# Rate of a convolution's taps and hold of three transposes in a decoder layer on one core

## The chip, the cores and the metric

The kernel runs on one core of a Trainium2 chip. The metric is device time in microseconds. Three runs of the kernel before took 1584.47 to 1587.35 us, with a median of 1585.04.

## The reference

One decoder layer on 256 tokens of width 2048, in float32:

```python
h = rmsnorm(x, g_mix); proj = h @ w_in
u_glu, q_da, k_da, v_da, q_xa, gate_pre = split(proj)
# branch A
u = a * sigmoid(b)                       # a, b: halves of u_glu, 1024 channels each
u = causal depthwise conv of u (31 taps) + b_dw
y_conv = silu(layernorm(u, g_ln, b_ln)) @ w_conv_out
# branch B: differential attention, 4 heads, rotary; branch C: cross-attention into rmsnorm(mem)
y_da = (...) @ w_da_out;  y_xa = (...) @ w_xa_out
merged = g0 * y_conv + g1 * y_da + g2 * y_xa      # g: sigmoid(gate_pre)
x = x + merged @ w_mix_out
x = x + square(relu(rmsnorm(x, g_mlp) @ w_up)) @ w_down     # d_ff 8192
out = rmsnorm(x, g_final)
```

## The kernel before

Every weight matrix is read once, in blocks of 256 rows by 512 columns. `produce` (L306) loads a block (`raw`, on SP's queue), ScalarE rounds it to `whi`, and VectorE makes the rest, `wlo`. There are four buffers of each. Activations are kept transposed and split in the same way (class `Act`), so that a product is three matmuls: hi by whi, hi by wlo, lo by whi (L346 to L348). A `group` (L334) multiplies one activation by 512 columns of a weight: 8 steps of one block each for 2048 rows, 4 for 1024. A step is 2 k-tiles by 2 token halves by 3 matmuls, 12 of 128x512. Up to three further blocks are produced ahead of the step at hand. Before the products of a k-tile the group calls `finish` on the task that makes that tile of the activation (L367), which issues whatever the task has left.

Side work is written as generators, the tasks, in four lanes ("t", "conv", "a0", "a1"). At the end of a step `side_step` (L137) gives the first task of each lane one `tick`. A tick adds the task's rate to its credit, and each whole unit of credit runs the task to its next yield. A task with hold=1 starts one unit short, so its first tick issues nothing (L86). A finished task leaves its lane, and the next one starts.

The lane "conv" carries, in this order, `conv_half(0)`, spawned at the end of the second w_in group, `conv_half(1)`, spawned at the end of the fourth (both at rate CONV_RATE), and `conv_norm` at NORM_RATE = 1 (L627). `conv_half` (L509) transposes its half of u through TensorE in four steps and then takes 31 steps of four VectorE operations, one tap on four channel blocks each. The taps are tied behind the last product issued so far (`later`, L525). `conv_norm` (L528) is the layer norm over channels and the swish: two reductions, a matmul with ones (`pm`), eight subtractions, eight squares with seven additions, a second matmul (`pvar`), square root, reciprocal and a Newton step, eight scalings, and for each of the eight channel blocks a sigmoid, an affine activation, their product and its split into cvT's hi and lo parts. It has 31 yields.

The order of the groups: four of w_in (the convolution's input), four of w_mem_kv, two of w_in for the cross-attention's q, four for q and k, two for v. Then, for each of four column chunks c: three gate groups, and the three branch outputs w_xa_out, w_da_out and w_conv_out (4 steps each), which read xaT, daT and cvT. The branch outputs are merged on VectorE (`products`, L879). Then four groups of w_mix_out on mT, and four times four groups of w_up on x1T and four of w_down on ff.

`to_parts_dve` (L248) turns a chunk of 512 columns round with 16 VectorE transposes of 32x256 in four steps, tied behind the last `wlo` issued (L245), and splits it in two more. It is spawned with HOLD = 1 for each merged chunk (L894), each chunk of x1 (in `x1_task`, L929) and each relu chunk (L959). The merged and x1 chunks are made by VectorE, the relu chunks by ScalarE (relu and square). When the last chunk of four is spawned, the very next group needs it at its seventh step of eight.

A planner orders each engine's instructions when the program is built, by the order of issue and a model of when each is ready. It may draw an instruction ahead of its place if nothing ties it.

```python
CONV_RATE = 0.6
...
            conv_tasks.append(spawn(conv_half(g), "conv", CONV_RATE))
...
    t_norm = spawn(conv_norm(), "conv", NORM_RATE)
    cvT.tasks = [t_norm] * 8
...
                finish(act.tasks[k + c])
```

Of the kernel before, what the change touches and what calls it, by code (L numbers as in the profile page):

```python
# [27 lines left out]
EPS = 1e-6  # L28
G = 512
KB = 2  # L30
CONV_RATE = 0.6
NORM_RATE = 1.0
WARM = 10
WB = 4
AHEAD = 3
HOLD = 1
LAMBDA_INIT = 0.8 - 0.6
NEG = -3.0e38
VECS = (("g_mix", 16), ("g_mem", 16), ("g_mlp", 16), ("b_dw", 8), ("g_ln", 8), ("b_ln", 8), ("g_sub", 2))
# [68 lines left out]
def decoder_layer_kernel(  # L108
# [19 lines left out]
    def spawn(gen, lane="t", rate=1.0, hold=0):  # L128
        t = Task(gen, rate, hold)
        lanes[lane].append(t)  # L130
        return t
# [64 lines left out]
    def both(f):  # L196
        seen = []

        def g(t, ps):
            seen.append(ps)  # L200
            if len(seen) == NT:
                f(seen)

        return g
# [13 lines left out]
    def scaled_parts(st, i, dst, kt, n, gname):  # L218

        his = [  # L220
            nc.scalar.activation(  # L221
                dst.hi(kt + c), st[:, i + c : i + c + 1, :], AF.Copy, scale=vcol(gname, kt + c)
            )
            for c in range(n)
        ]
        los = [
            nc.vector.scalar_tensor_tensor(
                dst.lo(kt + c), st[:, i + c : i + c + 1, :], vcol(gname, kt + c),
                dst.hi(kt + c).bitcast(F32), ALU.mult, ALU.subtract,
            )  # L230
            for c in range(n)
        ]
        return his[-1], los[-1]

    def block_transpose2(src, dst):

        B = 32
        out_v = dst.rearrange("p j (t s) -> p t j s", t=NT)
        in_v = src.rearrange("p t (j c k) -> p t j c k", c=P // B, k=B)
        for q in range(P // B):  # L240
            for c in range(P // B):
                ins = nc.vector.transpose(  # L242
                    out_v[c * B : (c + 1) * B, :, :, q * B : (q + 1) * B], in_v[q * B : (q + 1) * B, :, :, c, :]
                )
                later(ins, lo_mark[0])  # L245
            yield

    def to_parts_dve(src, dst, kt0, gname=None):  # L248

        st = work.tile([P, G // P, S], F32, tag="chunk", name="st", bufs=4)  # L250
        yield from block_transpose2(src, st)
        for b in range(0, G // P, 2):
            k = kt0 + b
            if gname is None:
                nc.scalar.copy(dst.hi(k, 2), st[:, b : b + 2, :])  # L255
                nc.vector.tensor_tensor(dst.lo(k, 2), st[:, b : b + 2, :], dst.hi(k, 2).bitcast(F32), op=ALU.subtract)
            else:
                scaled_parts(st, b, dst, k, 2, gname)
            yield
# [140 lines left out]
    def sum_rsqrt(ssum, dim, name):  # L400
        tot = const.tile([P, NT], F32, name=name + "_t")
        nc.vector.tensor_reduce(tot, ssum, AX.X, ALU.add)
        return rsqrt_of(tot, NT, dim, name)
# [105 lines left out]
    def conv_half(g):  # L509
        u = sig[g]  # L510
        yield from transpose_plain(by_tok(u), uT, g * 4, 4)
        cbs = range(g * 4, g * 4 + 4)
        for d in range(TAPS):
            for cb in cbs:
                i = (TAPS - 1 - d) * 8 + cb
                w = taps[:, i : i + 1]
                if d == 0:
                    ins = nc.vector.tensor_scalar(
                        conv[:, cb, :], uT[:, cb, :], w, vcol("b_dw", cb), ALU.mult, ALU.add
                    )  # L520
                else:
                    ins = nc.vector.scalar_tensor_tensor(  # L522
                        conv[:, cb, d:], uT[:, cb, : S - d], w, conv[:, cb, d:], ALU.mult, ALU.add
                    )
                later(ins, mark[0])  # L525
            yield
# [55 lines left out]
    def evac_a(g):  # L582
        def f(ps):
            for t in range(NT):
                nc.vector.scalar_tensor_tensor(
                    sig[g][:, t, :], ps[t], rinv["x"][:, t : t + 1], sig[g][:, t, :], ALU.mult, ALU.mult
                )
            conv_tasks.append(spawn(conv_half(g), "conv", CONV_RATE))
        return both(f)
# [286 lines left out]
    mT = Act(units, "mT", 16)  # L876
    NC4 = D // G

    def products(c):  # L879
        mg = work.tile([P, NT, G], F32, tag="chunk", bufs=4, name="mg")  # L880
        for j, (i, w, act) in enumerate(((2, w_xa_out, xaT), (1, w_da_out, daT), (0, w_conv_out, cvT))):
            def f(ps, i=i, j=j):
                for t in range(NT):
                    gt = gates[i, c][:, t, :]
                    if j == 0:
                        nc.vector.tensor_tensor(mg[:, t, :], ps[t], gt, op=ALU.mult)
                    else:
                        nc.vector.tensor_tensor(gt, ps[t], gt, op=ALU.mult)
                for t in range(NT):
                    gt = gates[i, c][:, t, :]  # L890
                    if j > 0:
                        nc.vector.tensor_tensor(mg[:, t, :], mg[:, t, :], gt, op=ALU.add)
            group(w, 0, c * G, act, both(f))
        tk = spawn(to_parts_dve(mg, mT, c * 4), hold=HOLD)  # L894
        mT.tasks[c * 4 : c * 4 + 4] = [tk] * 4

    for c in range(NC4):
# [17 lines left out]
    def x1_task(c):  # L915
        yield from to_parts_dve(x1c[c], x1T, c * 4, "g_mlp")
        for t in range(NT):
            junk = work.tile([P, G], F32, tag="t2k", name="junk", bufs=4)
            nc.scalar.activation(junk, x1c[c][:, t, :], AF.Square, accum_out=ss1[:, t, c : c + 1])
        if c == NC4 - 1:  # L920
            rinv["mlp"] = sum_rsqrt(ss1, D, "rinv_mlp")
        yield

    for c in range(NC4):
        def f(ps, c=c):
            for t in range(NT):
                xs = x1c[c][:, t, :]
                nc.vector.tensor_tensor(xs, ps[t], xs, op=ALU.add)
            tk = spawn(x1_task(c), hold=HOLD)  # L929
            x1T.tasks[c * 4 : c * 4 + 4] = [tk] * 4  # L930
        group(w_mix_out, 0, c * G, mT, both(f))

# [3 lines left out]
    def final_scale(t):  # L936
        tot = const.tile([P, 1], F32, name=f"tot{t}")
        nc.vector.tensor_reduce(tot, ss2[:, t, :], AX.X, ALU.add)
        rv = rsqrt_of(tot, 1, D, f"rinv_fin{t}")
        for c in range(NC4):  # L940
            xs = x1c[c][:, t, :]
            if c == NC4 - 1:
                nc.vector.scalar_tensor_tensor(xs, xs, rv, gfin[:, c * G : (c + 1) * G], ALU.mult, ALU.mult)
            elif c % 2 == 1:
                nc.scalar.activation(xs, xs, AF.Copy, scale=rv)
            else:
                nc.vector.tensor_scalar_mul(xs, xs, rv)
            nc.sync.dma_start(out[t * P : (t + 1) * P, c * G : (c + 1) * G], xs)

    for j in range(DFF // D):  # L950
        uu = Act(units, f"ff{j}", 16)
        for g in range(4):
            def f(ps, g=g, uu=uu):
                ru = work.tile([P, NT, G], F32, tag="chunk", bufs=4, name="ru")
                for t in range(NT):
                    nc.scalar.activation(ru[:, t, :], ps[t], AF.Relu, scale=rinv["mlp"][:, t : t + 1])
                for t in range(NT):
                    nc.scalar.activation(ru[:, t, :], ru[:, t, :], AF.Square)
                tk = spawn(to_parts_dve(ru, uu, g * 4), hold=HOLD)  # L959
                uu.tasks[g * 4 : g * 4 + 4] = [tk] * 4  # L960
            group(w_up, 0, j * D + g * G, x1T, both(f))
        for c in range(NC4):
            last = j == DFF // D - 1
            H = G // 2

            def f(t, ps, c=c, last=last):
                xs = x1c[c][:, t, :]
                if not last:
                    nc.vector.tensor_tensor(xs, ps, xs, op=ALU.add)
                    return  # L970
                for h in range(2):
                    hs = slice(h * H, (h + 1) * H)
                    nc.vector.tensor_tensor(xs[:, hs], ps[:, hs], xs[:, hs], op=ALU.add)
                for h in range(2):
                    hs = slice(h * H, (h + 1) * H)
                    junk = work.tile([P, H], F32, tag="t2k", name="junk", bufs=4)
                    i = 2 * c + h
                    nc.scalar.activation(junk, xs[:, hs], AF.Square, accum_out=ss2[:, t, i : i + 1])
                if c == NC4 - 1:
                    final_scale(t)  # L980
                else:
                    nc.vector.tensor_tensor(xs, xs, gfin[:, c * G : (c + 1) * G], op=ALU.mult)

            group(w_down, j * D, c * G, uu, f, split=3 if last and c == NC4 - 1 else 0)
# [45 lines left out]
```

## Time and profile before

| | us |
|---|---|
| median of three runs | 1585.04 |
| the profiled execution | 1584.57 |
| its span, first to last instruction | 1582.0 |
| TensorE busy | 1567.4 |
| VectorE busy | 1130.4 |
| ScalarE busy | 782.9 |
| GpSimd busy | 23.3 |

In the profile PE is TensorE's matmul, PEld its weight load, which runs beside matmuls, DVE is VectorE, ACT ScalarE, POOL GpSimd and SP the queue of the weight loads. A row of a timeline gives the start in us from the span's start, the duration in us, the engine, the line of the kernel, the operation, output and inputs by the program's names, and how many instructions it stands for; in brackets, the idle time before it and what ended that. Durations overlap on an engine, so the distance of two starts says how fast it goes.

### The profile page before, as it was taken

What the parts mean: (1) busy time and instruction counts of PE and PEld (TensorE: products, weight loads), DVE (VectorE), ACT (ScalarE), POOL (GpSimd) and SP (SyncE); (2) the same over time, 40 slices, a digit from 0 to 9 for tenths busy, and PEclk for the clock granted to TensorE, in tenths of its full rate; (3) what the DMA queues carried; (4) which work ended last, traced back from release to release, by engine and by line L of the source; (5) the groups of instructions that cost most, each with busy time, mean ns of one, the idle gap of its engine ahead of it and who ended that gap; (6) DMA issues with size and microseconds to landing.
All of it is one profiled execution on the core that took longest, in us unless ns stands there. A gap on an engine that the chain in (4) does not pass through costs nothing.

```text
span 1582.0 us, 18995 instructions
## 1 busy us (share of the span) xinstructions
PE 1567.4 (99%) x6956; PEld 1296.6 (82%) x6956; DVE 1130.4 (71%) x1639; ACT 782.9 (49%) x1007; POOL 23.3 (1%) x35
## 2 busy tenths in 40 slices
PE   9999999999999999999999999999999999999997
PEld 7888788888888888888888788888888888888886
DVE  5699998887877456474598798447864687548864
ACT  7655445454784444444444555335534454445543
POOL 1000000010000000000000000000000000000000
PEclk9999999999999999999999999999999999999999
DMA  9776575556556666667766666666666666666663
GB/s 345 238 247 193 154 219 162 154 151 200 152 172 195 198 192 196 192 192 207 260 188 199 186 195 188 197 194 190 195 195 192 187 196 197 192 197 187 194 195 129
DMA packets 158732, 308.93 MB, mean 195 GB/s; under 512 B 9792, under 2 KB 10048, under 8 KB 158512
## 3 DMA queue, kind: packets, MB, share of 16 engines
q1 hardware_dynamic: 157104, 303.60, 63.0%
q0 software_dynamic: 960, 3.57, 0.8%
q8 instruction: 54, 0.88, 0.2%
q10 hardware_dynamic: 576, 0.56, 0.1%
q14 instruction: 38, 0.31, 0.1%
HBM read 305.60 MB, written 2.10 MB: 194 GB/s over the span
## 4 chain that ended last, share of the span: by engine, by line
PE 95%; DVE 3%; issue 1%; ACT 0%; DMA 0%; POOLq 0%; POOL 0%; ACTq 0%; DVEq 0%
PE acc L346 31%; PE acc L347 31%; PE acc L348 31%; DVE wlo L326 1%; DVE kxT L242 1%; DVE conv L522 1%; PE xs L678 0%; PE xo L711 0%; DVE st L242 0%; PE ds L773 0%; PE do L824 0%; PE tr L173 0%; DMA xt<-in_x_t_dram 0%; ACT whi L325 0%; PE xpt L173 0%
## 5 line engine op out<-in xcount | busy, mean ns | idle before, releaser
L326 DVE TENSOR_TENSOR wlo<-raw,whi 128x1024 fp32r<-128x1024 f32 (+1 forms) x561 | 684.4, 1221 | 413.0 <-ACT whi L325 409.0
L325 ACT CAST whi<-raw 128x1024 fp32r<-128x1024 f32 (+1 forms) x561 | 589.8, 1052 | 689.5 <-PE acc L348 641.7
L347 PE MATMUL acc<-wlo,xT_hi 128*128 128x512 f32 x768 | 300.2, 392 | 1.0 <-DVE wlo L326 1.0
L346 PE MATMUL acc<-whi,xT_hi 128*128 128x512 f32 x768 | 298.3, 395 | 2.8 <-ACT whi L325 2.8
L348 PE MATMUL acc<-whi,xT_lo 128*128 128x512 f32 x768 | 298.7, 392 | 0.0
L346 PE MATMUL acc<-whi,x1T_hi 128*128 128x512 f32 x512 | 198.2, 389 | 1.1 <-ACT x1T_hi L221 1.1
L347 PE MATMUL acc<-wlo,x1T_hi 128*128 128x512 f32 x512 | 199.0, 389 | 0.0
L346 PE MATMUL acc<-whi,ff_hi 128*128 128x512 f32 x512 | 198.7, 390 | 0.0
L347 PE MATMUL acc<-wlo,ff_hi 128*128 128x512 f32 x512 | 198.6, 389 | 0.0
L348 PE MATMUL acc<-whi,x1T_lo 128*128 128x512 f32 x512 | 198.4, 389 | 0.0
L348 PE MATMUL acc<-whi,ff_lo 128*128 128x512 f32 x512 | 197.9, 389 | 0.0
L346 PEld LDWEIGHTS acc<-whi,xT_hi 128*128 128x128 f32 x768 | 144.7, 189 | 32.7 <-ACT whi L325 3.0
L347 PEld LDWEIGHTS acc<-wlo,xT_hi 128*128 128x128 f32 x768 | 144.5, 188 | 31.3 <-DVE wlo L326 2.1
L348 PEld LDWEIGHTS acc<-whi,xT_lo 128*128 128x128 f32 x768 | 144.5, 188 | 29.9
L242 DVE STREAM_TRANSPOSE st<-ru 32x256 f32<-32x256 f32 x256 | 111.6, 436 | 4.1
L346 PEld LDWEIGHTS acc<-whi,x1T_hi 128*128 128x128 f32 x512 | 96.1, 188 | 21.5 <-ACT x1T_hi L221 1.6
L346 PEld LDWEIGHTS acc<-whi,ff_hi 128*128 128x128 f32 x512 | 96.1, 188 | 21.1 <-ACT ff_hi L255 1.4
L347 PEld LDWEIGHTS acc<-wlo,x1T_hi 128*128 128x128 f32 x512 | 96.1, 188 | 20.1 <-DVE wlo L326 0.2
L348 PEld LDWEIGHTS acc<-whi,ff_lo 128*128 128x128 f32 x512 | 96.1, 188 | 20.0
L347 PEld LDWEIGHTS acc<-wlo,ff_hi 128*128 128x128 f32 x512 | 96.1, 188 | 19.9
L348 PEld LDWEIGHTS acc<-whi,x1T_lo 128*128 128x128 f32 x512 | 96.1, 188 | 19.9
L522 DVE SCALAR_TENSOR_TENSOR conv<-uT,taps,conv 128x255 f32<-128x255 f32 (+29 forms) x240 | 98.2, 461 | 0.3
(197 smaller groups left out, 1376.0 us busy)
## 6 DMA issues: line engine op xcount, KB each, us to landing
raw<-in_w_in_dram SPq DMA_DIRECT2D x191, 512.0 KB, 4.3
raw<-in_w_up_dram SPq DMA_DIRECT2D x128, 512.0 KB, 3.8
raw<-in_w_down_dram SPq DMA_DIRECT2D x128, 512.0 KB, 4.7
raw<-in_w_mem_kv_dram SPq DMA_DIRECT2D x32, 512.0 KB, 4.6
raw<-in_w_mix_out_dram SPq DMA_DIRECT2D x32, 512.0 KB, 4.7
raw<-in_w_xa_out_dram SPq DMA_DIRECT2D x16, 512.0 KB, 4.8
raw<-in_w_da_out_dram SPq DMA_DIRECT2D x16, 512.0 KB, 4.7
raw<-in_w_conv_out_dram SPq DMA_DIRECT2D x16, 512.0 KB, 4.7
```

The lines of the kernel that those rows point to most:

```text
L242: ins = nc.vector.transpose(out_v[c * B : (c + 1) * B, :, :, q * B : (q + 1) * B], in_v[q * B : (q + 1) * B, :, :, c, :])
L325: hi = nc.scalar.copy(whi[:, cs, :], raw[:, cs, :])
L326: lo_mark[0] = nc.vector.tensor_tensor(wlo[:, cs, :], raw[:, cs, :], whi[:, cs, :].bitcast(F32), op=ALU.subtract)
L346: nc.tensor.matmul(ps[t], hi[:, tt], whi[:, c, :], start=kt == 0, stop=False)
L347: nc.tensor.matmul(ps[t], hi[:, tt], wlo[:, c, :], start=False, stop=False)
L348: return nc.tensor.matmul(ps[t], lo[:, tt], whi[:, c, :], start=False, stop=kt == nkt - 1)
L522: ins = nc.vector.scalar_tensor_tensor(conv[:, cb, d:], uT[:, cb, : S - d], w, conv[:, cb, d:], ALU.mult, ALU.add)
```

## The change

The convolution's rate goes from 0.6 to 0.5, so that a half's task takes one step in every second tick. The hold of one tick is dropped for the merged chunks, for x1's chunks and for the last of four relu chunks; the other three relu chunks keep it.

```diff
--- before.py
+++ after.py
@@ -28,12 +28,11 @@
 EPS = 1e-6
 G = 512
 KB = 2
-CONV_RATE = 0.6
+CONV_RATE = 0.5
 NORM_RATE = 1.0
 WARM = 10
 WB = 4
 AHEAD = 3
-HOLD = 1
 LAMBDA_INIT = 0.8 - 0.6
 NEG = -3.0e38
 VECS = (("g_mix", 16), ("g_mem", 16), ("g_mlp", 16), ("b_dw", 8), ("g_ln", 8), ("b_ln", 8), ("g_sub", 2))
@@ -891,7 +890,7 @@
                     if j > 0:
                         nc.vector.tensor_tensor(mg[:, t, :], mg[:, t, :], gt, op=ALU.add)
             group(w, 0, c * G, act, both(f))
-        tk = spawn(to_parts_dve(mg, mT, c * 4), hold=HOLD)
+        tk = spawn(to_parts_dve(mg, mT, c * 4))
         mT.tasks[c * 4 : c * 4 + 4] = [tk] * 4
 
     for c in range(NC4):
@@ -926,7 +925,7 @@
             for t in range(NT):
                 xs = x1c[c][:, t, :]
                 nc.vector.tensor_tensor(xs, ps[t], xs, op=ALU.add)
-            tk = spawn(x1_task(c), hold=HOLD)
+            tk = spawn(x1_task(c))
             x1T.tasks[c * 4 : c * 4 + 4] = [tk] * 4
         group(w_mix_out, 0, c * G, mT, both(f))
 
@@ -956,7 +955,7 @@
                     nc.scalar.activation(ru[:, t, :], ps[t], AF.Relu, scale=rinv["mlp"][:, t : t + 1])
                 for t in range(NT):
                     nc.scalar.activation(ru[:, t, :], ru[:, t, :], AF.Square)
-                tk = spawn(to_parts_dve(ru, uu, g * 4), hold=HOLD)
+                tk = spawn(to_parts_dve(ru, uu, g * 4), hold=1 if g < 3 else 0)
                 uu.tasks[g * 4 : g * 4 + 4] = [tk] * 4
             group(w_up, 0, j * D + g * G, x1T, both(f))
         for c in range(NC4):
```

## Rows read from the trace of the kernel before

**Rows 1.** Busy time, share of the span and instructions of each engine (the page, part 1).

```profile
PE 1567.4 (99%) x6956; PEld 1296.6 (82%) x6956; DVE 1130.4 (71%) x1639; ACT 782.9 (49%) x1007; POOL 23.3 (1%) x35
```

**Rows 2.** Waits of TensorE (PE) and its weight loads (PEld): total us, times, longest.

```profile
PE acc L346 <- ACT x1T_hi L221: 1.1, 1, 1.1
PE acc L347 <- DVE wlo L326: 1.0, 2, 0.8
PEld acc L346 <- ACT ff_hi L255: 1.4, 4, 0.3
PEld acc L346 <- ACT mT_hi L255: 0.3, 1, 0.3
```

**Rows 3.** Timeline of PE inside a gate group: start us, duration us, instruction.

```profile
499.81 0.39 PE L347 MATMUL acc<-wlo,xT_hi 128*128 128x512 f32 x1
500.04 0.39 PE L348 MATMUL acc<-whi,xT_lo 128*128 128x512 f32 x1
```

**Rows 4.** Timelines of DVE and PE: the norm's reductions, pm, pvar, w_conv_out's first product.

```profile
405.37 3.91 DVE L536 TENSOR_REDUCE lnt<-conv 128x128 f32<-128x1024 f32 x2
418.38 0.59 PE L538 MATMUL pm<-lnt,ones 128*128 128x256 f32 x2
441.77 0.59 PE L554 MATMUL pvar<-lnt,ones 128*128 128x256 f32 x2
482.58 0.39 PE L346 MATMUL acc<-whi,cvT_hi 128*128 128x512 f32 x1
```

**Rows 5.** Timeline of DVE where w_conv_out begins.

```profile
484.69 1.22 DVE L326 TENSOR_TENSOR wlo<-raw,whi 128x1024 fp32r<-128x1024 f32 x1
```

**Rows 6.** Timelines of DVE and ACT: operations of conv_norm, in order.

```profile
419.17 2.73 DVE L541 TENSOR_TENSOR conv<-conv,pm 128x256 f32<-128x256 f32 x8
443.77 1.28 ACT L557 ACT_TABLE_LOAD   x1
445.06 0.42 ACT L557 ACTIVATE lnt<-lnt 128x256 f32<-128x256 f32 x1
445.52 1.75 DVE L559 RECIPROCAL lnt<-lnt 128x256 f32<-128x256 f32 x1 [1.24 <-ACT lnt L557]
447.30 0.42 DVE L561 TENSOR_TENSOR lnt<-lnt 128x256 f32<-128x256 f32 x1
452.13 0.60 ACT L573 ACTIVATE sg<-conv,vec 128x256 f32<-128x256 f32 x1
452.64 0.59 ACT L575 ACTIVATE y<-conv,vec 128x256 f32<-128x256 f32 x1
455.78 0.40 ACT L578 CAST cvT_hi<-y 128x256 fp32r<-128x256 f32 x1
```

**Rows 7.** The kernel's first table load (groups by line; last: idle before it, releaser).

```profile
L221 ACT ACT_TABLE_LOAD x1 | 1.3, 1283 | 5.4 <-DMA xt<-in_x_t_dram 5.4
```

**Rows 8.** Weight casts (the page, part 5: busy us, mean ns | idle before).

```profile
L325 ACT CAST whi<-raw 128x1024 fp32r<-128x1024 f32 (+1 forms) x561 | 589.8, 1052 | 689.5 <-PE acc L348 641.7
```

**Rows 9.** Timeline of DVE: transposes of xqT.

```profile
232.83 7.18 DVE L242 STREAM_TRANSPOSE xqT<-xq 32x256 f32<-32x256 f32 x16
```

**Rows 10.** Timelines of ACT and DVE: squares and transposes of relu's last chunk.

```profile
964.86 1.14 ACT L958 ACTIVATE ru<-ru 128x512 f32<-128x512 f32 x2
968.22 1.78 DVE L242 STREAM_TRANSPOSE st<-ru 32x256 f32<-32x256 f32 x4
```

**Rows 11.** Transposes of the two conv halves (tile sig; ns min/median/max, first and last start us).

```profile
L173 PE MATMUL tr<-ident,sig x16: 270/272/273, 58.3 to 180.2; 128*128 128x128 f32 x16
```

**Rows 12.** TensorE's start: stretch with busy times and granted clock (third from last); then timeline.

```profile
8.00:10.00 2.00, 2.00 (x5) 1.49 (x5) 1.27 (x3) 1.45 (x3) 0.00 (x0) 0.50 1.05 404
7.71 1.22 PE L346 MATMUL acc<-whi,xT_hi 128*128 128x512 f32 x2 [2.77 <-ACT whi L325]
9.16 0.63 PE L348 MATMUL acc<-whi,xT_lo 128*128 128x512 f32 x1
9.59 0.63 PE L347 MATMUL acc<-wlo,xT_hi 128*128 128x512 f32 x1
```

## The prediction

> **What bounds the kernel now.** I read the page's busy times first: TensorE is busy for 99% of the span [rows 1]. Then its waits, to see what it lost: in the middle of the kernel it waited 1.1 us for x1T and 1.0 us for wlo, and its weight loads waited 1.4 us in all for ff (four times) and 0.3 us for mT [rows 2]. Then the stream itself: products start 0.23 us apart [rows 3], so one step of two weight tiles (12 products) is 2.72 us. I call such a step a tick: group ends each with side_step, which gives every lane one tick. So there is almost nothing to win: all the waits above are 3.8 us, 0.24% of the time. There is a lot to lose wherever TensorE is made to wait, and the question is which side work has a due time that the change moves.
>
> **Conv at rate 0.5: the count.** A conv_half has 35 yields (4 for the transposes, 31 for the taps) and ends on its 36th step. The two halves share one lane, and conv_norm follows them there at rate 1. Count ticks from the end of the second w_in group, where the first half is spawned. From there to the first w_conv_out group lie 14 groups of 8 ticks (two of w_in, four of w_mem_kv, two for xq, four for q and k, two for v), three gate groups (24) and two branch groups of 4: 144 ticks. At 0.6 a half takes 36/0.6 = 60 ticks, both take 120, and conv_norm gets 24 of its 31 steps before w_conv_out. The trace agrees: the reductions that open conv_norm run at 405.4 us, its first matmul (pm, third step, tick 123) at 418.4 and its second (pvar, tenth step, tick 130) at 441.8 [rows 4]. From tick 130 to 144 are 14 ticks, 38.1 us, and w_conv_out's first product is at 482.6 [rows 4], 40.8 us later; the difference is the attention heads' own matmuls. At 0.5 a half takes 72 ticks and both take 144. The last taps are issued at tick 142 and conv_norm gets no tick at all. Its 31 steps are then issued in one go by the finish in front of w_conv_out's first product, which needs cvT. Before, its last seven steps were left by then, the planner had drawn them ahead, and TensorE shows no wait there [rows 2]; now the whole norm stands between the last attention product and w_conv_out.
>
> **What can cover it.** The reductions, some 4 us, can still run beside the second branch group: they ran straight behind the last taps before, and the taps end two ticks before that group does. TensorE has nothing else to do: the blocks behind w_conv_out's four need a whi buffer, there are four of those, and w_conv_out's four blocks hold them until its products have run. So the rest is exposed.
>
> **Its length**, from where w_conv_out began. VectorE first finishes the second branch's merge and then one wlo, which starts at 484.69 and takes 1.2 us [rows 5], so it comes to the norm 3.3 us in (pm is ready after 0.8 us, so without these two it would be 2.5 us less). Eight subtractions 2.7 us [rows 6], seven additions of the same kind at 0.34 us: 2.4. pvar to its reader: the two matmuls take 0.6 [rows 4]. The variance, an operation of 128x256, 0.4 [rows 6]. A table load 1.3 and the square root 0.5 until the reciprocal starts; the reciprocal 1.8; four small operations at 0.42: 1.7; the first scaling 0.4; another table load 1.3; sg and y 1.1; their product 0.4; the cast to cvT_hi 0.4 [rows 6]. Sum: 3.3 + 2.7 + 2.4 + 0.6 + 0.4 + 1.8 + 1.8 + 1.7 + 0.4 + 1.3 + 1.1 + 0.4 + 0.4 = 18.3 us. The table loads I count in full: the first one of the kernel stood waiting for its activation's input, 5.4 us for a DMA [rows 7], so a load doesn't run ahead; if it did, 2.6 us less. After the first tile ScalarE sets the pace: sg, y and the cast start 0.51, 0.5 and 0.3 us apart, 1.3 us a tile [rows 6], and three weight casts of 1.05 us [rows 8] come between as buffers come free. The last of eight tiles is ready 18.3 + 7 x 1.3 + 3.2 = 30.6 us in, and 6 more products end the group at 32.0. Unhindered its 48 products take 10.9. The loss is 21.1 us, less 0.9 for pm and pvar, which no longer stand inside the gate groups: **20.2 us**. With both loads hidden, the norm ahead of the merge, and no weight casts between: 11.9. The upper end is the second rival.
>
> A page would set the table loads higher. In the trace a load is 1.28 us, it follows 0.02 us behind the activation before it, and the square root starts 0.01 us behind it [rows 6]. The Trainium skill's page "ScalarE: Activation LUTs", section "What ACT_TABLE_LOAD costs", adds a drain of about the load's own length to every switch of tables; by it the sum would be some 2.8 us more. The row shows no such pause, and the row decides.
>
> **Conv at rate 0.5: the load on VectorE.** Fewer taps per tick lie beside the transposes of kxT, where wlo was late, so I take TensorE's 1.0 us back [rows 2]. What is late next: the first half's taps now last to tick 70 instead of 59, over the transposes of xqT, of which 16 run in one stretch of 7.2 us at 232.8 [rows 9]. Three further blocks stand ready, 8.2 us of products. They cover the stretch as they do now, unless taps add to it: nothing, with up to 2 us.
>
> **The holds.** A spawned transpose now starts one tick, 2.7 us, earlier. For x1's last chunk that is more than its 1.1 us wait, which goes; mT's 0.3 and ff's 1.4 go with it [rows 2]: 2.8 us in all, and no more can come from this part. Where the next group doesn't read the chunk (merged chunks 0 to 2, x1 chunks 0 to 2) nothing waits for the transposes, and the hold is worth nothing. No DMA moves: SP's loads follow the buffers, and nothing is put on POOL. For relu's last chunk the added wait is on VectorE: transposes one tick after the group would start about 965.5, the squares end at 966.0 [rows 10], so the wlo behind them is up to 0.5 us late. Three blocks ready cover that. Without the cover it costs 4 x 0.5 = 2 us, which is the bad end.
>
> **Sum.** The profiled execution took 1584.57 us (span 1582.0, 2.6 around it), 0.47 below the median. 1584.6 + 20.2 - 1.0 - 2.8 = **1601 us**. Least: 1584.6 + 11.9 - 3.8 = 1592.7. With 20.2 and neither gain, plus 2 + 2: 1608.8.
>
> **Rivals.** First, **not slower: TensorE's order is changed so that the next gate group fills the gap.** For it: the instructions don't stand in program order. The second half's transposes are due at ticks 62 to 67, after 215 us, and the last of them ran at 180.2 [rows 11]. Against it: those needed only ready data and a free PSUM tile, while a gate product needs a cast block, and all four buffers are taken. It decides from the point where one block behind w_conv_out could be cast before w_conv_out's first product. Then the norm is hidden and only the gains are left: 1584.6 - 3.8 = 1580.8, just past the bound of what a measurement can tell from no change, 0.2% or 3.2 us; with half of the gains it is no change. 10%.
>
> Second, **slower still: w_conv_out runs at half clock.** At the start TensorE waited 2.8 us, the granted clock from 8 to 10 us was then 0.50 (1.2 of 2.4 GHz), and products came 0.43 us apart [rows 12]. Here it waits for far longer, so it starts slow; I took it that the clock comes back within the group and stays hidden behind ScalarE's pace. If it doesn't, the 48 products take 20.6 us from 18.3 on, the loss is 18.3 + 20.6 - 10.9 - 0.9 = 27.1, and the time 1584.6 + 27.1 - 3.8 = 1608; to 1612 without the gains. The Trainium skill's page "TensorE: Matmul & The Clock Gate", section "HAM oscillation — how this bites in real kernels", describes a kernel that waits for data between short bursts and runs each burst throttled. Nothing in this trace has bursts to test that on; here a wait between tiles is under 1 us. 13%.
>
> Third, **the norm is partly hidden**: the last taps and the reductions run far enough ahead that more than the reductions falls beside the second branch. The taps are tied to the product in front of them in the order of issue, so at most the two ticks, 5.4 us, come to the 4 I gave them, and with the 2.6 and 2.5 us of the bounds above the loss is 9.7 us, and 6.5 if the weight casts stay out of the way as well: 1587 to 1591. 5%.
>
> **How the numbers follow.** The forecast, an exposed norm of 12 to 23 us, has 72%; second rival 13%; third 5%; first 10%, half of it faster and half the same. Slower 0.90, same 0.05, faster 0.05. The range 1592 to 1612 holds the forecast and the second rival, 85%.
>
> **What would show it.** Right: in the profile after, a wait of TensorE for cvT_hi or for the norm's DVE operations, 15 to 20 us in front of w_conv_out's first product and nowhere else; pm, pvar, the square root and all eight sg in one stretch between the second branch and w_conv_out; a clock near 0.5 where it resumes; later stages shifted by the same 20 us; the waits for x1T and ff gone. Wrong: pm issued well before the second branch's products end, gate products between, or a stall under 10 us. If TensorE waits for wlo near 240 us, the tap load was mis-sized; if it waits for wlo at the start of the w_down groups, the hold was.

## The result and the profile after

The changed kernel takes 1604.75 us (median of four runs, 1603.32 to 1605.28) against 1585.49 for the kernel before: a ratio of 1.0115, with a 95% interval of 1.0103 to 1.0128. The prediction was slower, 1601 us, within 1592 to 1612. The profiled execution took 1603.32 us and its span is 1600.8, against 1584.57 and 1582.0.

Line numbers after are one lower than before, since a constant is gone. The page of the changed kernel: busy times, then, of the 40 slices, TensorE's busy share in tenths and its granted clock in tenths of full speed.

```profile
PE 1569.4 (98%) x6956; PEld 1297.7 (81%) x6956; DVE 1134.1 (71%) x1639; ACT 785.0 (49%) x1007; POOL 19.8 (1%) x35
...
PE   9999999999995999999999999999999999999997
...
PEclk9999999999997999999999999999999999999999
```

The busy times are those of before within 4 us [rows 1]; no engine has more to do. What is new is a single slice, the 13th, in which TensorE is busy for half of the time and its clock dips. One slice is 40 us, 480 to 520. Then TensorE's waits after, which answer to [rows 2], without those of the first 8 us (total us, times, longest):

```profile
PE pvar L553 <- DVE lnt L549: 9.2, 1, 9.2
PE acc L345 <- ACT cvT_hi L577: 8.7, 1, 8.7
...
PE acc L346 <- DVE wlo L325: 0.9, 2, 0.5
```

Two waits are new, one in front of pvar and one for the first cvT tile, 17.8 us together (9.19 and 8.65 in the timeline below). The wait for x1T is gone, and the weight loads' waits for ff and mT no longer stand in their list. The wait for wlo is still there, 0.9 us where it was 1.0. The timeline of PE after shows where the new ones stand (start, duration, instruction, in brackets the wait), and how the products come after them:

```profile
482.19 0.40 PE L347 MATMUL acc<-whi,daT_lo 128*128 128x512 f32 x1
482.42 0.59 PE L537 MATMUL pm<-lnt,ones 128*128 128x256 f32 x2
492.20 1.22 PE L553 MATMUL pvar<-lnt,ones 128*128 128x256 f32 x2 [9.19 <-DVE lnt L549]
502.08 0.79 PE L345 MATMUL acc<-whi,cvT_hi 128*128 128x512 f32 x1 [8.65 <-ACT cvT_hi L577]
...
503.10 0.63 PE L345 MATMUL acc<-whi,cvT_hi 128*128 128x512 f32 x1
503.52 0.63 PE L346 MATMUL acc<-wlo,cvT_hi 128*128 128x512 f32 x1
...
506.61 0.39 PE L345 MATMUL acc<-whi,cvT_hi 128*128 128x512 f32 x1
506.83 0.39 PE L346 MATMUL acc<-wlo,cvT_hi 128*128 128x512 f32 x1
...
510.69 0.62 PE L345 MATMUL acc<-whi,xT_hi 128*128 128x512 f32 x2
```

pm follows the second branch's last product at once. Before, pm ran at 418.38 and pvar at 441.77 [rows 4]; now the whole norm stands between the second branch and w_conv_out. Products start 0.43 us apart at first and 0.22 to 0.23 from about 505.7 on. At 510.69, with cvT tiles still to come, two products of the next gate group go in between.

**Where the time went**, by the starts of products. From the first product of w_xa_out of chunk 0 to the one of chunk 1 is a stretch that holds w_conv_out once. The first pair of rows is from the timeline of before, the second from the one after:

```profile
460.82 0.39 PE L346 MATMUL acc<-whi,xaT_hi 128*128 128x512 f32 x1
558.74 0.39 PE L346 MATMUL acc<-whi,xaT_hi 128*128 128x512 f32 x1
```

```profile
460.65 0.39 PE L345 MATMUL acc<-whi,xaT_hi 128*128 128x512 f32 x1
580.05 0.39 PE L345 MATMUL acc<-whi,xaT_hi 128*128 128x512 f32 x1
```

The stretch takes 97.92 us before and 119.40 after: 21.5 us more. Ahead of it several small changes, taken apart in the part on the prediction, add up to a start 0.2 us earlier. Behind it, up to the end of the span, 1023.3 became 1020.8: 2.5 us less. 21.5 - 0.2 - 2.5 is the 18.8 us by which the spans differ. I call this stretch the w_conv_out stretch and use it below, because the first 100 us of an execution vary by up to 3 us from run to run while the stretch repeats to 0.01 us where nothing in it is touched.

### The profile page after: what moved, and what is told of

Its sections match the earlier page's. It is cut to its first block, busy times and chain, and to the rows that moved or that the text cites. A ratio compares the mean times of both kernels' runs of the same rounds, so it can differ in the third digit from the quotient of the medians.

```text
span 1600.8 us, 19000 instructions
## 1 busy us (share of the span) xinstructions
PE 1569.4 (98%) x6956; PEld 1297.7 (81%) x6956; DVE 1134.1 (71%) x1639; ACT 785.0 (49%) x1007; POOL 19.8 (1%) x35
## 4 chain that ended last, share of the span: by engine, by line
PE 95%; DVE 3%; issue 1%; ACT 1%; DMA 0%; POOLq 0%; DVEq 0%; POOL 0%; ACTq 0%
PE acc L345 31%; PE acc L346 31%; PE acc L347 31%; DVE wlo L325 1%; PE xo L710 0%; PE xs L677 0%; DVE xqT L241 0%; PE tr L172 0%; PE ds L772 0%; PE do L823 0%; DVE conv L521 0%; DMA xt<-in_x_t_dram 0%; DVE kxT L241 0%; DVE lnt L549 0%; DVE conv L540 0%
```

## Experiments

**1. The rate alone, and the holds alone.** The first keeps the holds, the second keeps the rate.

```diff
-CONV_RATE = 0.6
+CONV_RATE = 0.5
```

> The convolution at 0.5, the three holds kept as before. If the whole slowdown is the late layer norm of the convolution and the dropped holds only take short waits away: TensorE stands for about 9 us in front of pvar and 9 us in front of w_conv_out's first product as in the changed kernel, and its waits for x1T_hi (1.1 us) and of its weight loads for ff_hi (1.4 us) are there again; the time is the changed kernel's 1604.75 plus 2.5, 1607.2 us. Rival, that the dropped holds have a part in the slowdown: below 1604.

> The convolution at 0.6 as before, the holds dropped. Late norm theory: no wait in front of w_conv_out, the waits for x1T_hi, ff_hi and mT_hi gone, 2.5 us less than before: 1583.0 us. Rival, that transposes one step earlier hold up wlo on VectorE: new waits of TensorE for wlo at the start of w_mix_out, w_up or w_down and 1585.5 us or more.

The rate alone takes 1607.94 us, ratio 1.0141 (1.0125 to 1.0156). Its two waits in front of pvar and w_conv_out are those of the changed kernel, and the waits that the holds made are back (waits of PE, then of PEld):

```profile
PE pvar L554 <- DVE lnt L550: 9.2, 1, 9.2
PE acc L346 <- ACT cvT_hi L578: 8.7, 1, 8.7
...
PE acc L346 <- ACT x1T_hi L221: 1.2, 1, 1.2
...
PEld acc L346 <- ACT ff_hi L255: 1.4, 4, 0.3
```

The holds alone take 1583.58 us, ratio 0.9984 (0.9975 to 0.9992), and behind the first 27 us all that TensorE waits for is this:

```profile
PE acc L346 <- DVE wlo L325: 1.0, 2, 0.8
```

So the holds gain about 2 us and the rate costs about 22. Both are where the theory had them. The w_conv_out stretch with the holds alone is 97.92 us again.

**2. A slower first half, with the norm on time.**

```diff
-CONV_RATE = 0.5
+CONV_RATES = (0.5, 0.75)
...
-            conv_tasks.append(spawn(conv_half(g), "conv", CONV_RATE))
+            conv_tasks.append(spawn(conv_half(g), "conv", CONV_RATES[g]))
```

> The changed kernel, with the first conv half at 0.5 and the second at 0.75: 72 + 48 = 120 ticks, so the norm starts at tick 121 as before. Due time theory: the slower rate costs nothing by itself, pm runs near 418 us and nothing waits in front of w_conv_out; as the holds alone, 1583 us within 1. Rival, that the slower taps of the first half cost by what they collide with on VectorE around 190 to 250 us: 1585 to 1588 with waits of TensorE for wlo there.

It takes 1583.56 us, ratio 0.9988 (0.9979 to 0.9996): the time of the holds alone. In its timeline of PE the norm is on time again (everything is 3.3 us later in this execution, 3.0 of it already by the fourth w_in group, as w_xa_out's first product shows, at 464.12):

```profile
421.67 0.59 PE L537 MATMUL pm<-lnt,ones 128*128 128x256 f32 x2
```

The w_conv_out stretch is 97.92 us, as before. The first half ran at 0.5 as in the changed kernel. From the first product of the fourth w_in group to that of the second gate group this execution took 334.11 us against 333.77 before, so the slower half cost 0.3 us there and nothing in the stretch. What costs is the norm's start, 24 ticks later in the changed kernel. This is the run that separates the due time from the rate.

**3. Other lengths of lateness: 0.55 and 0.45.** Only the constant differs.

> The changed kernel at rate 0.55: a half takes 66 ticks, both 132, and the norm gets 12 of its 31 steps before w_conv_out, so pvar is issued at tick 142, two ticks ahead. Due time theory: what follows pvar, some 10 us to the first cvT tile, is 5 to 7 us longer than the two ticks, TensorE waits once, for cvT_hi, and not for pvar; 1585.5 - 2.5 + 5 to 9 (with a slow clock after the wait): 1588 to 1592 us. Rival, that the cost goes with the rate evenly between 0.6 (1583) and 0.5 (1604.75): 1594 us.

> The changed kernel at rate 0.45: 80 ticks a half, so 7 of the second half's tap steps (1.4 us each) and the two reductions (4 us) are issued behind the second branch's end as well, in front of the norm. Due time theory: the wait in front of pm, pvar and cvT's first product grows by 14 to 16 us, 1620 us. Rival, that the time goes evenly with the rate, about 10 us for each 0.05: 1615 us.

The medians are 1594.88 and 1615.33 us, ratios 1.0056 (1.0044 to 1.0069) and 1.0188 (1.0174 to 1.0202). Both numbers came out at the rival's, so the times alone don't tell the theories apart. The waits do. At 0.55, behind the first 25 us, there are two:

```profile
PE acc L345 <- ACT cvT_hi L577: 8.3, 1, 8.3
...
PE acc L346 <- DVE wlo L325: 1.6, 1, 1.6
```

and at 0.45 three new ones:

```profile
PE pm L537 <- DVE lnt L535: 14.6, 1, 14.6
PE acc L345 <- ACT cvT_hi L577: 8.7, 1, 8.7
PE pvar L553 <- DVE lnt L549: 6.3, 1, 6.3
```

At 0.55 pvar was in time and only what follows it stood exposed. The wait for wlo there is another matter: it stands at 246.5 us, behind 16 transposes of xqT in one stretch of 7.2 us. No other run has one of that size at this place, and none tells whether the rate made it. At 0.45 the taps and the reductions stand in front of pm as well. That is the due time's pattern, and its sizes were off. At 0.55 I had 5 to 7 us for the wait and it was 8.3. The timeline of DVE shows what held it up:

```profile
482.38 1.75 DVE L558 RECIPROCAL lnt<-lnt 128x256 f32<-128x256 f32 x1 [0.51 <-ACT lnt L556]
484.17 0.43 DVE L560 TENSOR_TENSOR lnt<-lnt 128x256 f32<-128x256 f32 x1
...
485.98 1.28 DVE L887 TENSOR_TENSOR gate<-acc,gate 128x512 f32<-128x512 f32 x2
...
489.12 0.68 DVE L891 TENSOR_TENSOR mg<-mg,gate 128x512 f32<-128x512 f32 x1
489.72 0.42 DVE L563 TENSOR_TENSOR lnt<-lnt 128x256 f32<-128x256 f32 x1
```

The second branch's merge and two wlo fall into the middle of the Newton step, which takes from 484.17 to 490.14 instead of 1.7 us. The w_conv_out stretch is 108.95 us at 0.55 and 132.47 at 0.45, against 119.40 in the changed kernel and 97.92 before. At 0.45 I had 14 to 16 us more than the changed kernel and it is 13.1: the merge's operations ran between the last taps (the last of them starts at 489.39, pm at 498.58), so that they no longer stand between pm and pvar, which are 7.6 us apart there instead of 9.8.

**4. The table load taken out of the chain.** The extra Sigmoid reads the square root's result, so its load runs behind it.

```diff
         nc.scalar.activation(std, var, AF.Sqrt)
+        nc.scalar.activation(warm, std[:, 0:1], AF.Sigmoid)
```

> The changed kernel with one tiny Sigmoid right behind the square root, so that the second table load runs while VectorE still works on the reciprocal. Theory of a single exposed chain: the 1.28 us load leaves the chain (in the changed kernel it began only when the first scaling was done), the wait for cvT_hi goes from 8.7 to 7.4 us and the time from 1604.75 to 1603.5 us. Rival, that the load is covered or that another engine paces the chain: 1604.7, same wait.

The wait for cvT_hi fell from 8.7 to 8.0 us, half of what I had, and the stretch from 119.40 to 119.16. The median is 1603.02 us (ratio to before 1.0109, 1.0095 to 1.0123); that interval overlaps with the changed kernel's, so the stretch decides, and it says 0.2 us. The chain itself gave 0.6: from pm to w_conv_out's first product are 19.0 us instead of 19.7. The rest went behind that product, where products stood 0.43 us apart for 4.4 us instead of 3.6; this is the slow clock of experiment 5. The timeline of ACT of this run:

```profile
495.19 0.42 ACT L556 ACTIVATE lnt<-lnt 128x256 f32<-128x256 f32 x1 [2.14 <-DVE lnt L555]
495.63 1.28 ACT L557 ACT_TABLE_LOAD   x1
496.92 0.20 ACT L557 ACTIVATE warm<-lnt 128x1 f32<-128x1 f32 x1
...
502.27 0.40 ACT L578 CAST cvT_hi<-y 128x256 fp32r<-128x256 f32 x1 [0.60 <-DVE y L577]
```

The load is out of the way, and the next thing is late in its place: the cast waits 0.6 us for VectorE's product of y and sg, which stands behind all eight scalings. My theory of one chain was too simple. At this point ScalarE and VectorE run nearly level, and a microsecond off one is not a microsecond off the end.

**5. TensorE kept at work during the wait.** The products go to a spare tile that nothing reads; the same lines stand behind pvar.

```diff
         nc.tensor.matmul(pm, ones, nwt, start=True, stop=True)
+        dummy = psum.tile([P, S], F32, tag="tr", name="dummy")
+        for _ in range(70):
+            nc.tensor.matmul(dummy, ones.bitcast(F32R), xT.hi(0)[:, 0, :], start=True, stop=True)
```

> The changed kernel with 70 products of 128x256 into a spare PSUM tile behind pm and 70 behind pvar, work that nothing reads, to keep TensorE from standing. Theory that the slow clock behind the wait is a cost of its own, since gate products fill in where cvT tiles are late: the granted clock stays at 1.0, the products of w_conv_out come 0.23 us apart from the first one on, and 1.9 us are saved: 1602.8 us. Rival, the prediction's, that the slow start hides behind ScalarE's pace: 1604.7. If the filling itself delays pvar or cvT's products: above 1605.

The stretch fell to 117.44 us, 2.0 less than the changed kernel's. The median is 1603.10 us, 1.65 less; the ratio to before, 1.0109 (1.0095 to 1.0123), doesn't by itself set it apart. A window of the changed kernel around w_conv_out's first product, and then the same one of this run (window, its length, busy times of PE, PEld, DVE, ACT and POOL, granted clock as a share of 2.4 GHz, DMA share, GB/s):

```profile
502.00:504.00 2.00, 1.92 (x5) 1.54 (x6) 1.38 (x4) 2.00 (x6) 0.00 (x0) 0.50 0.00 0
```

```profile
502.00:504.00 2.00, 1.50 (x13) 1.30 (x13) 1.29 (x5) 2.00 (x6) 0.00 (x0) 1.00 0.00 0
```

So of the 21.5 us about 2 are the slow clock, and they are not hidden. Half a microsecond of them lies ahead of w_conv_out's first product (from pvar to it, 9.4 us instead of 9.9), the other 1.5 behind it.

**6. The wait for wlo, and a kernel faster than both.** The holds dropped, the rate 0.6, and the rotary tables in the empty lane a1 instead of ahead of the transposes of kx.

```diff
-    t_tables = spawn(tables())
+    t_tables = spawn(tables(), "a1")
```

> The kernel with the holds dropped and the rate 0.6, and the rotary tables moved from the lane of the transposes to the lane a1, which is empty then. If TensorE's wait for wlo near 193 us comes from eight transposing steps in a row behind the tables, not from the taps' rate: those of the first kx chunk move some 15 to 20 ticks earlier, the two waits (1.0 us) go, and 1.3 us are saved against 1583.6: 1582.3 us. Rival, that it hangs on the taps beside them: the waits stay, or move with the transposes, and the time stays at 1583.6.

It takes 1582.02 us, ratio to before 0.9978 (0.9968 to 0.9988), the fastest of all. TensorE's waits for wlo fell from 1.0 us to 0.4, and what is left moved with the transposes, from 192.6 and 196.4 us with the holds alone to 163.5:

```profile
PE acc L346 <- DVE wlo L325: 0.4, 1, 0.4
```

So the wait hangs on where the transposing steps stand. That the taps' rate has no part in it isn't shown: at 0.55 there is no wait for wlo near 193 us at all. Against the holds alone the medians differ by 1.6 us, more than the wait explains. From the first product of the fourth w_in group to that of the second gate group this execution took 332.88 us against 333.78, 0.9 less; the rest is not told apart from the spread of the start.

## Why the prediction was right

**The count was right, and it decided.** 144 ticks, none left for the norm: pm at 482.42, directly behind the second branch's last product. The chances followed from it.

**The length of the norm** was forecast as 21.1 us in the w_conv_out stretch; it is 21.5. This agreement holds errors of both signs, so that it is so close is luck. The timeline of DVE after, from the second branch's end:

```profile
482.38 1.27 DVE L887 TENSOR_TENSOR gate<-acc,gate 128x512 f32<-128x512 f32 x2
...
484.17 2.73 DVE L540 TENSOR_TENSOR conv<-conv,pm 128x256 f32<-128x256 f32 x8
486.82 0.68 DVE L891 TENSOR_TENSOR mg<-mg,gate 128x512 f32<-128x512 f32 x1
487.42 1.22 DVE L325 TENSOR_TENSOR wlo<-raw,whi 128x1024 fp32r<-128x1024 f32 x1
488.56 0.41 DVE L549 TENSOR_TENSOR lnt<-sq 128x256 f32<-128x256 f32 x1
489.07 3.07 DVE L549 TENSOR_TENSOR lnt<-lnt,sq 128x256 f32<-128x256 f32 x6
493.46 0.42 DVE L555 TENSOR_SCALAR lnt<-pvar 128x256 f32<-128x256 f32 x1 [1.31 <-PE pvar L553]
```

The merge and one wlo did come in between, as forecast, but around the subtractions rather than all ahead of them. The additions took 3.6 us, not 2.4: each reads the one before, and they start about 0.5 us apart, while I had priced them by the subtractions [rows 6], which are independent of each other and start 0.33 us apart. pvar took 0.6 us longer to reach its reader than before: TensorE's granted clock had already fallen to 0.50, and with the clock kept up (experiment 5) most of this goes. The timeline of ACT after shows both table loads:

```profile
490.50 1.28 ACT L556 ACT_TABLE_LOAD   x1
493.92 0.42 ACT L556 ACTIVATE lnt<-lnt 128x256 f32<-128x256 f32 x1 [2.14 <-DVE lnt L555]
498.36 1.28 ACT L572 ACT_TABLE_LOAD   x1 [4.03 <-DVE conv L566]
499.66 0.60 ACT L572 ACTIVATE sg<-conv,vec 128x256 f32<-128x256 f32 x1
```

The first ran ahead, two microseconds before its activation had its input; the second waited, as the kernel's first one does [rows 7]. I had counted both, so this term is 1.3 us too large. Behind it the first cast waits for two blocks' sg and y. In all the first product came 19.7 us after the second branch's end; I had 18.3.

**The end of the group** is where the sum gave most of that back. I let ScalarE's tiles set the pace up to 32.0 us and held that nothing could fill in, since the four whi buffers are taken. The pace was as forecast: the last of the eight casts to cvT_hi ends at 512.91, 30.5 us in, where I had 30.6.

```profile
512.50 0.41 ACT L577 CAST cvT_hi<-y 128x256 fp32r<-128x256 f32 x1 [0.83 <-DVE y L576]
```

But TensorE doesn't wait for it: behind w_conv_out's first product no wait is left in the stretch. That nothing could fill in holds in front of that product and failed after it: each finished step frees a buffer, and from 510.69 on gate products ran while cvT tiles were late. So the 2.8 us that I had for the pace fell away, and 1.8 us stand in their place, of the eight first products, which were slow: 19.7 + 1.8 = 21.5, where I had 18.3 + 2.8 = 21.1. For the same reason the step "I took it that the clock comes back within the group and stays hidden behind ScalarE's pace" is wrong in its second part. The clock did come back, within 4 us of the first product, but what it cost, 2.0 us (experiment 5), showed. The second rival, half clock throughout, is out. The page's picture of bursts that each run throttled (the Trainium skill, "TensorE: Matmul & The Clock Gate", "HAM oscillation — how this bites in real kernels") isn't met here either: there is one slow stretch, it ends at 505.7, and there is no return to it while TensorE had gate products to fill in. With the rate alone, the same two waits were followed by a slow clock that lasted 5.3 us instead of 3.6, and the stretch took 120.21 us instead of 119.40. There the granted clock, in this view of the same form as in experiment 5, is still 0.50 from 506 to 508 us, where it was 1.00 in the changed kernel:

```profile
506.00:508.00 2.00, 2.00 (x6) 1.51 (x6) 1.05 (x3) 2.00 (x6) 0.00 (x0) 0.50 0.00 0
```

The rule set against the sum, a drain added to every table load (the Trainium skill, "ScalarE: Activation LUTs", "What ACT_TABLE_LOAD costs"), isn't borne out here either: in experiment 4 the load starts 0.02 us behind the square root, and the next activation 0.01 us behind the load.

**The holds** were put at 2.8 us and gave 2.5 behind the w_conv_out stretch. The bad end, wlo held up behind relu's squares, was 0.5 us a chunk; the wait is there, 0.4 us each, and no product waited for it (waits of DVE after):

```profile
DVE st L241 <- ACT ru L957: 1.6, 4, 0.4
```

**The taps' relief** failed: "fewer taps per tick lie beside the transposes of kxT, where wlo was late, so I take TensorE's 1.0 us back". The wait stayed at 0.9, and the way up to the second gate group became longer instead of shorter. Its first product, before and after:

```profile
409.30 0.39 PE L346 MATMUL acc<-whi,xT_hi 128*128 128x512 f32 x1
```

```profile
410.09 0.39 PE L345 MATMUL acc<-whi,xT_hi 128*128 128x512 f32 x1
```

Of the 0.8 us between them, 0.3 are there by the fourth w_in group and belong to the spread of the start. From that group's first product on it was 333.77 us before and is 334.28 now, 0.5 more. With the rate alone it is 334.24 and with the holds alone 333.78, so the rate of 0.5 did it; it doesn't go on growing as the rate falls, for at 0.45 it is 333.55. The allowance of up to 2 us, where the taps meet the transposes of xqT, is the term it belongs to, and the sign named for it shows there, on a weight load:

```profile
245.79 0.19 PEld L346 LDWEIGHTS acc<-wlo,xT_hi 128*128 128x128 f32 x1 [0.56 <-DVE wlo L325]
```

What else makes up the 0.5 us I did not trace. The 0.9 us of pm and pvar, which left the gate groups, came as forecast: from the product above to w_xa_out's first one, 51.52 us became 50.57. So the distance from 16.4 us forecast to 18.8 between the two profiled executions is the relief that turned into a cost (1.5), the norm (0.4), the holds (2.5 instead of 2.8) and the start (0.3), less 0.1 for pm and pvar.

**The signs.** TensorE's waits, the clock and the shift of the later stages came as named. One sign came in part: of the eight sg only three start ahead of w_conv_out's first product, the others beside its products. And gate products between, named as a sign of being wrong, did come, but behind that product and not ahead of it.

The first rival had the right sign of doubt: TensorE's order did change, and it filled part of the group, but it couldn't fill the wait itself. The third was not seen: the reductions ended before pm's place, and nothing more was drawn ahead.

## What to carry to other kernels

Where side work is metered out by steps, count the steps up to where each result is needed, and then count what follows it in the same lane: here the convolution itself was in time at the lower rate, and its norm got no step at all. An engine that is busy for 99% of the span leaves almost nothing to win, so ask of any change which due time it moves. Times that lie evenly on a line can hide a mechanism with steps; compare the list of waits, and a stretch between two fixed products, rather than the medians.

## What was not expected of the hardware

Of two table loads in the changed kernel, one ran ahead of its activation's input by 2.1 us; the other stood 4.0 us until the input was there. At 0.55 that same load ran ahead, by 2.5 us; no run shows what decides it. Additions of 128x256 on VectorE of which each reads the one before start about 0.5 us apart, where independent subtractions start 0.33 apart; that the dependence is the reason was not tested. After the same two waits the slow clock lasted 3.6 us in one execution and 5.3 in another.
